# The first mixer of an encoder trunk: eight q buffers, an earlier fourth q projection, LayerNorm's scale and shift behind the spatial product, one 1/std chain for three blocks

## The chip, the cores and the metric

The kernel runs on one core of a Trainium2 chip. The metric is the device time of one execution in microseconds (us), as the median over several executions; a lower time is better. A core has a matrix engine (TensorE, PE in the profile, with its weight load as PEld), three engines for elementwise work (VectorE or DVE, ScalarE or ACT, GpSimd or POOL) and a queue from which the transfers here are issued (SyncE, SP). Each engine works through its own list of instructions in order and waits at an instruction whose operands or buffers are not there yet.

## The reference

Two groups of tokens, a prompt of 512 and a sample of 256, go through two layers with shared weights; the width is D = 1024. Each layer is a half SwiGLU, a mixer and a second half SwiGLU. The change is in the mixer of the first layer alone, which computes, with h the normed input:

```python
z = h @ w_in
zs = jax.nn.gelu(z[..., :2 * SGU_WIDTH], approximate=False)
u, vh = zs[..., :SGU_WIDTH], zs[..., SGU_WIDTH:]            # 512 each
vh = layer_norm(vh, sgu_ln_g, sgu_ln_b)                     # (x - mu) * rsqrt(var + EPS) * g + b
vh = vh.reshape(B, nc, BLOCK, SGU_GROUPS, SGU_GROUP_DIM)    # blocks of 128 tokens, 4 groups of 128
vmix = jnp.einsum('gij,bnjgc->bnigc', sgu_w, vh) + jnp.transpose(sgu_b)[None, None, :, :, None]
a_out = u * vmix.reshape(B, L, SGU_WIDTH)
...
b_out = window_gqa(rope_partial(q), rope_partial(k), v, sink)
return jnp.concatenate([a_out, b_out], axis=-1) @ w_out
```

`window_gqa` is attention of 8 query heads over 2 key and value heads (kv 0 and 1): each block of 128 queries looks at its own block and its two neighbours within its group, through a mask, with a softmax that has one more term for each head, the sink. The results are float32 and must be exact to about that.

## The kernel before, in words

**Arithmetic.** A float32 operand is split into a rounded high part and a rest ("hi" and "lo": `split`, L194 to L197, a cast on ACT at L196 and a subtraction on DVE at L197). A product takes three matmuls, hi with hi, hi with lo, lo with hi (`mm3`, L176), all issued at L140. One such group of three is called a step below. `proj` (L183) makes a projection as eight steps, one for each 128 rows of D. Weights arrive as `raw` by DMA on the SP queue (L92) and are split in halves of 512 columns into `whi` (ACT, L114) and `wlo` (DVE, L115), with five buffers of each. Transposes on PE are issued at L144.

**Layout.** All 768 tokens lie in one axis: columns 0 to 512 are the prompt (four blocks of 128), 512 to 768 the sample (two blocks). `GROUPS` cuts it there, `HALVES` in 384 and 384. PSUM has two pools with four banks each: "mm" for projections, "aux" for everything short.

**What sets the order.** PE's list is the order in which the program issues matmuls; the program keeps a virtual time `self.t`, to which each matmul adds its estimated length (L134). Side work is written as generators that yield a delay: `spawn` (L146) adds one, and `tick` (L158), called after each step, runs those whose time has come, so their matmuls stand between the steps of a projection. `run_until` and `drain` (L164, L172) step the generators at once, whatever their delay, until something is reached. The lists of ACT, DVE, POOL and SP are made by a list scheduler that takes instructions as their operands become ready by its own model of time; they are fixed in the program and do not adapt on the chip. A buffer of a pool is given out in the order of the program's requests.

**The first mixer** (`mixer0`, L927 to L1144). It loads tables (rope, mask `msk`, `sink`, LayerNorm's gain `lng` and shift `lnb`, both spread over all partitions, the spatial product's offset `sb`) and the spatial weights, which it splits into `swh` and `swl` (L952). It projects keys and values for both groups (L983). `roped` (L959) rotates a projection out of PSUM in four DVE steps with two buffers of the pool "tmp". This pool has three buffers of 128 x 512, shared by the rotation (`rt`, `ru`), the values (`vf`), the copies of value products (`tb`), the gate's tiles (`vg`), those of u (`ug`) and the raw spatial weights.

- `q_heads(m)` (L998) projects two query heads for both groups, rotates them and splits them into q tiles: for each group a pool with six buffers, of which one `q_heads` takes two (hi and lo). There are four such calls.
- `attention` (L1061) is the generator for the softmax part. For each kv and each of the six blocks it issues scores (`score`, L1008, whose softmax is `finish_rows`, L900: row maximum on DVE L907, exp on ACT L913, the sink's part L918, reciprocal, product with 1/sum on DVE L922), yields `GAP0`, issues the value product of the block before (`values`, L1048: copy on ACT, four adds on DVE), yields `GAP0` again, and transposes and splits the probabilities (`turn`, L1032). kv 0 needs the q tiles of calls 0 and 1, kv 1 those of calls 2 and 3. "Score (0,5)" is the last block of kv 0.
- `vh_part` (L1109) projects the gate half for two groups of three blocks, each block in an mm bank, with tokens as partitions. Each result goes through the exact Gelu on ACT (L1121) into a "tmp" tile, and a generator `sgu` is spawned for it.
- `sgu` (L1079) is LayerNorm and the spatial product of one block: statistics (L1082, L1085), 1/std by a chain of 13 small DVE steps (`rsqrt`, L262 to L276), then three DVE passes over 128 x 512 (subtract mean and times 1/std L1087, times gain L1090, plus shift L1091), a split (L1095), twelve matmuls of 128 columns on `swh` and `swl`, and four adds of `sb` on DVE (L1105). The delays between are `SGU`.
- `u_part` (L1124) projects the other half, multiplies by the token norm, applies Gelu and multiplies into the spatial product's result.
- The main part (L1137 to L1144) spawns the attention, calls `q_heads` 0 to 2 and `vh_part`, then steps the generators until score (0,5) has been issued (L1141), calls `q_heads(3)` and `u_part`, and ends with `mixer_out` (L821). There `ready(k)` splits the mixer's result (L833) for the output projection, six of eight tiles ahead of it, the last two after the attention has been drained.

ACT loads another function table (`ACT_TABLE_LOAD`) where its list changes between Gelu and Exp.

Of the kernel before, what the change touches and what calls it, by code (L numbers as in the profile page):

```python
# [42 lines left out]

WTOTAL = 12 * D * FF + 8 * EARLY * P * D + D * 1792 + 2 * D * D + D * 3072 + D * 512
VTOK = (4.0,9.0)
GAP0 = 5.4
SGU = (8.0, 3.0, 4.0)
NP, NQ = 16, 2
GAPS1 = (3.5, 0.6, 3.5, 0.8)
# [2 lines left out]
class Trunk:  # L52
# [874 lines left out]
    def mixer0(self):  # L927
        nc = self.nc
        mp = self.mixer_open("m0")
        self.spawn(self.norm_r(mp, False))  # L930
        xs = (self.xh, self.xl)
        tmp = lambda name: mp.tile([P, TA], F32, tag="tmp", name=name, bufs=3)
# [6 lines left out]
        nc.sync.dma_start(msk, self.aps["gmask"])  # L939
        sink = mp.tile([P, P], F32, tag="sink", name="sink")[:, :8]  # L940
        nc.sync.dma_start(sink, self.aps["sink"].partition_broadcast(P))
        lng = mp.tile([P, 512], F32, tag="lng", name="lng")
        nc.sync.dma_start(lng, self.aps["ln_g"].partition_broadcast(P))
        lnb = mp.tile([P, 512], F32, tag="lnb", name="lnb")
        nc.sync.dma_start(lnb, self.aps["ln_b"].partition_broadcast(P))
        sb = mp.tile([P, 512], F32, tag="sb", name="sb")
        nc.sync.dma_start(sb, self.aps["sgu_b"].partition_broadcast(P))
# [2 lines left out]
        swh = mp.tile([P, 4, P], F32R, tag="swh", name="swh")  # L950
        swl = mp.tile([P, 4, P], F32R, tag="swl", name="swl")
# [7 lines left out]
        def roped(ps, c0, c1):  # L959
            n = c1 - c0  # L960
            t, u = tmp("rt")[:, :n], tmp("ru")[:, :n]
            nc.vector.stream_shuffle(out=u, in_=ps[:, :n], mask=swap)
            nc.vector.tensor_tensor(out=t, in0=ps[:, :n], in1=rct[:, c0:c1], op=ALU.mult)
# [21 lines left out]
        for g in (0, 1):  # L985
            c0, c1 = GROUPS[g]
            t = roped(pkv[g][0], c0, c1)
            for h in (0, 1):
# [3 lines left out]
                out=vf[:, : c1 - c0], in0=pkv[g][1][:, : c1 - c0], in1=self.rt[:, c0:c1], op=ALU.mult  # L992
# [3 lines left out]
        ot = [self.otile(k) for k in range(KD)]  # L996

        def q_heads(m):  # L998
            qs = []
            w = self.unit("l0_w_in", 0, KD, 1024 + m * P, P)  # L1000
            for g in (0, 1):
                c0, c1 = GROUPS[g]
                t = roped(self.proj(w, xs, GROUPS[g]), c0, c1)
                qs.append([mp.tile([P, c1 - c0], F32R, tag=f"q{g}", name=f"q{g}", bufs=6) for _ in "hl"])
                self.q_split(*qs[g], t)
            qheads.append(qs)

# [51 lines left out]
        qheads, scored, gates = [], [], []  # L1059

        def attention(gap):  # L1061
            cur = None
            for kv in (0, 1):
                for n in range(6):
                    while len(qheads) < 2 * kv + 2:
                        yield 0.5
                    new = score(kv, qheads[2 * kv : 2 * kv + 2], n)
                    scored.append((kv, n))
                    yield gap
                    if cur:  # L1070
                        values(*cur[:3], tt)
                    yield gap
                    cur = new
                    tt = turn(*cur)
                    yield 0.3 * gap
            yield 1.0
            values(*cur[:3], tt)

        def sgu(n, v):  # L1079

            bs = mp.tile([P, 6], F32, tag="bs", name="bs", bufs=2)
            nc.vector.bn_stats(out=bs, in_=v)  # L1082
            mv = mp.tile([P, 8], F32, tag="mv", name="mv", bufs=2)
            it = mp.tile([P, 1], I32, tag="mvi", name="mvi", bufs=2)
            nc.vector.bn_aggr(out=mv[:, 0:2], in_=bs)  # L1085
            self.rsqrt(mv[:, 2:3], mv[:, 1:2], 1.0, mv[:, 3:4], mv[:, 4:5], it)
            nc.vector.tensor_scalar(  # L1087
                out=v, in0=v, scalar1=mv[:, 0:1], scalar2=mv[:, 2:3], op0=ALU.subtract, op1=ALU.mult
            )
            nc.vector.tensor_tensor(out=v, in0=v, in1=lng, op=ALU.mult)  # L1090
            nc.vector.tensor_tensor(out=v, in0=v, in1=lnb, op=ALU.add)  # L1091
            yield SGU[0] + n % 3 * SGU[1]
            vh = mp.tile([P, 512], F32R, tag="vhh", name="vhh", bufs=2)
            vl = mp.tile([P, 512], F32R, tag="vhl", name="vhl", bufs=2)
            self.split(vh, vl, v)  # L1095
            yield SGU[2]
            ps = self.psum(self.aux, "aux")
            for g in range(4):
                c = slice(g * P, (g + 1) * P)
                self.mmul(ps[:, c], vh[:, c], swh[:, g, :], True, False)  # L1100
                self.mmul(ps[:, c], vh[:, c], swl[:, g, :], False, False)
                self.mmul(ps[:, c], vl[:, c], swh[:, g, :], False, True)
            for g in range(4):
                c = slice(g * P, (g + 1) * P)
                nc.vector.tensor_tensor(  # L1105
                    out=ot[g][:, n * P : (n + 1) * P], in0=ps[:, c], in1=sb[:, c], op=ALU.add
                )

        def vh_part():  # L1109
            for n0 in (0, 3):  # L1110
                ps = [self.psum() for _ in range(3)]
                for k in range(KD):
                    if k % 2 == 0:
                        w = self.unit("l0_w_in", k, 2, 512, 512)
                    for i in range(3):
                        a, b = (n0 + i) * P, (n0 + i + 1) * P
                        st = (self.xh[k][:, a:b], self.xl[k][:, a:b])
                        self.mm3(ps[i], st, w[k % 2], k == 0, k == KD - 1)
                for i in range(3):
                    v = tmp("vg")  # L1120
                    nc.scalar.activation(v, ps[i], AF.Gelu, scale=self.ry[:, n0 + i : n0 + i + 1])  # L1121
                    gates.append(self.spawn(sgu(n0 + i, v)))

        def u_part():  # L1124
            for m in range(4):
                w = self.unit("l0_w_in", 0, KD, m * P, P)
                for g in (0, 1):
# [6 lines left out]
                        self.drain(c)  # L1134
                    nc.vector.tensor_tensor(out=ot[m][:, c0:c1], in0=ot[m][:, c0:c1], in1=u, op=ALU.mult)

        att = self.spawn(attention(GAP0))  # L1137
        for m in range(3):
            q_heads(m)
        vh_part()  # L1140
        self.run_until(lambda: (0, 5) in scored)  # L1141
        q_heads(3)
        u_part()
        self.mixer_out("l0_w_out", ot, att)  # L1144
# [350 lines left out]
def trace(nc, phases=PHASES):  # L1495

    aps = {}
    inp = lambda n, s: aps.__setitem__(n, nc.dram_tensor(f"in_{n}", s, F32, kind="ExternalInput").ap())
    inp("x", (KD, P, T))
    inp("w", (WTOTAL,))  # L1500
    inp("gains", (P, KD * len(NORMS)))
    inp("rope", (2, P, TA))
    inp("gmask", (P, 3 * P))
    inp("nmask", (P, NMASK))
    inp("sink", (8,))
    inp("ln_g", (512,))
# [12 lines left out]

def layout(units, i):  # L1520
    x = np.concatenate([i["x_prompt"][0], i["x_sample"][0]], axis=0)
    w = np.zeros(WTOTAL, np.float32)
    off = 0
    for name, k0, nk, c0, n in units:
        size = P * nk * n
        w[off : off + size].reshape(P, nk, n)[...] = (
            i[name][k0 * P : (k0 + nk) * P, c0 : c0 + n].reshape(nk, P, n).transpose(1, 0, 2)
        )
        off += size
    rpb = np.zeros((16, 15, RPB_W), np.float32)  # L1530
    rpb[:, :, RPB_PAD : RPB_PAD + 31] = i["l1_rpb"]
    return {
        "in_x": np.ascontiguousarray(x.T).reshape(KD, P, T),
        "in_w": w,
        "in_gains": np.ascontiguousarray(np.concatenate([i[n].reshape(KD, P).T for n in NORMS], axis=1)),
        "in_rope": rope_tables(),
        "in_gmask": gqa_mask(),
        "in_nmask": natten_masks(),
        "in_sink": np.ascontiguousarray(i["l0_sink"]),
        "in_ln_g": np.ascontiguousarray(i["l0_sgu_ln_g"]),  # L1540
        "in_ln_b": np.ascontiguousarray(i["l0_sgu_ln_b"]),
        "in_sgu_b": np.ascontiguousarray(i["l0_sgu_b"].reshape(512)),
        "in_sgu_w": np.ascontiguousarray(i["l0_sgu_w"].transpose(2, 0, 1)),
        "in_rpb": rpb,
    }
# [21 lines left out]
```

## Time and profile before

| what | value |
|---|---|
| three executions | 2618.2, 2620.6 and 2620.9 us, median 2620.62 |
| the profiled execution | 2616.48 us in all, 2614.7 us span of its instructions |
| granted TensorE clock, mean | 0.991 |
| DMA | 218.99 MB, mean 84 GB/s |
| first mixer's stretch from gate projection to output projection, 580 to 696 us | PE busy 105.2 of 116 us, DVE 103.7, ACT 73.8 |
| rest of the span, 0 to 580 and 696 to 2614.7 us | PE busy 2447.9 of 2498.7 us |

All moments are microseconds from the start of the profiled span. A row of an instruction gives its start, its length in us, the engine, the line of the kernel, the operation, what it writes and reads by the program's names, its shape and how many of the same kind follow each other in the row; in brackets stands the time that the engine was idle just before and the instruction that ended this wait. A row of a group starts with its line and gives the count, then shortest, middle and longest length in ns, and the stretch in which they lie. A matmul's length is modelled and overlaps the next one, so that the step from one start to the next is the better measure of its cost. The granted clock is the TensorE clock as a share of full speed.

### The profile page before, as it was taken

Reading aid. Unit: us, or ns where it says so; the run is one execution under the profiler, and the core shown is the slowest. Engines: PE = TensorE matmul, PEld = TensorE weight load, DVE = VectorE, ACT = ScalarE, POOL = GpSimd, SP = SyncE. Lnnn points to the kernel's source line nnn. Section 1 sums busy time; section 2 is a strip of 40 time slices with the busy share of each in tenths; the row PEclk is TensorE's granted clock in tenths of the full one; section 3 lists DMA queues with packets and bytes.
Section 4 is the critical chain, followed back from the end, with each engine's and each line's share of the span. In section 5 each row is a group of like instructions: output and inputs, shape, how many; then the busy total and the mean of one; then the engine's idle time right before and its main releaser. Section 6 shows DMA issues by size and latency. Waiting matters only on the chain.

```text
span 2614.7 us, 41195 instructions
## 1 busy us (share of the span) xinstructions
PE 2553.1 (98%) x15094; PEld 2488.8 (95%) x15094; DVE 2264.1 (87%) x4793; ACT 1366.3 (52%) x2851; POOL 88.4 (3%) x172
## 2 busy tenths in 40 slices
PE   7999999998999999999999999999999999999997
PEld 7999999987899999999999999989898999999997
DVE  8998899889779989889999888986677699988897
ACT  7544454555655545445654445454445475444543
POOL 0000000000100000000000000001222100000000
PEclk9999999999999999999999999999999999999999
DMA  5333222421223322222322222232221332222221
GB/s 172 112 112 95 81 65 65 160 73 45 82 77 97 97 65 81 66 81 81 97 81 81 74 72 73 72 129 63 63 64 40 106 99 88 81 73 73 73 69 69
DMA packets 83898, 218.99 MB, mean 84 GB/s; under 512 B 20080, under 2 KB 32880, under 8 KB 83696
## 3 DMA queue, kind: packets, MB, share of 16 engines
q1 hardware_dynamic: 83552, 216.34, 26.3%
q8 instruction: 118, 1.93, 0.3%
q14 instruction: 84, 0.69, 0.1%
q10 hardware_dynamic: 144, 0.03, 0.0%
HBM read 206.90 MB, written 15.07 MB: 85 GB/s over the span
## 4 chain that ended last, share of the span: by engine, by line
PE 88%; DVE 8%; ACT 2%; issue 1%; DMA 1%; SPq 0%; DVEq 0%; ACTq 0%
PE ps_mm L140 55%; PE ps_aux L140 32%; DVE wlo L115 1%; PE ps_aux L144 1%; DMA raw<-in_w 1%; DVE xl L741 1%; ACT p L913 1%; DVE p L922 0%; DVE p L907 0%; DVE tl L197 0%; DVE tmp L362 0%; ACT xh L740 0%; DVE x L708 0%; DVE ol L197 0%; ACT whi L114 0%
## 5 line engine op out<-in xcount | busy, mean ns | idle before, releaser
L114 ACT CAST whi<-s 128x512 fp32r<-128x512 f32 x496 | 305.1, 620 | 413.7 <-DVE s L611 169.9
L114 ACT CAST whi<-raw 128x512 fp32r<-128x512 f32 x512 | 311.4, 618 | 232.5 <-PE ps_mm L140 98.7
L115 DVE TENSOR_TENSOR wlo<-s,whi 128x512 fp32r<-128x512 f32 x496 | 337.4, 686 | 56.3 <-ACT whi L114 53.9
L115 DVE TENSOR_TENSOR wlo<-raw,whi 128x512 fp32r<-128x512 f32 x494 | 337.7, 691 | 24.9 <-ACT whi L114 20.7
L140 PE MATMUL ps_mm<-db,whi 128*128 128x384 f32 x864 | 219.3, 334 | 0.4 <-DVE sg L508 0.4
L140 PE MATMUL ps_aux<-dt,whi 128*128 128x384 f32 x864 | 219.1, 334 | 0.0
L140 PEld LDWEIGHTS ps_mm<-db,whi 128*128 128x128 f32 x864 | 155.9, 188 | 0.7 <-DVE sg L508 0.7
L140 PEld LDWEIGHTS ps_aux<-dt,whi 128*128 128x128 f32 x864 | 156.0, 188 | 0.0
L140 PE MATMUL ps_mm<-xh,whi 128*128 128x512 f32 (+1 forms) x416 | 147.3, 354 | 3.6 <-ACT xh L740 3.6
L140 PE MATMUL ps_mm<-db,wlo 128*128 128x384 f32 x432 | 144.3, 334 | 0.0
L140 PE MATMUL ps_aux<-dt,wlo 128*128 128x384 f32 x432 | 144.3, 334 | 0.0
L140 PE MATMUL ps_mm<-xl,whi 128*128 128x512 f32 (+1 forms) x416 | 142.3, 342 | 1.1 <-DVE xl L741 1.1
L140 PE MATMUL ps_mm<-xh,wlo 128*128 128x512 f32 (+1 forms) x416 | 141.9, 341 | 0.0
L611 DVE TENSOR_TENSOR s<-raw,raw 128x512 f32<-128x512 f32 x124 | 84.0, 686 | 21.3 <-DMA raw<-in_w 21.1
L611 DVE TENSOR_TENSOR s<-raw 128x512 f32<-128x512 f32 x124 | 85.2, 687 | 18.6 <-DMA raw<-in_w 18.3
L499 DVE TENSOR_TENSOR u<-ps_aux,u 128x384 f32<-128x384 f32 x176 | 97.2, 552 | 4.0 <-PE ps_aux L140 3.9
L140 PE MATMUL ps_aux<-dh,whi 128*128 128x384 f32 x384 | 97.7, 335 | 0.6 <-DVE x L708 0.6
L913 ACT ACTIVATE p<-p,st 128x256 f32<-128x256 f32 (+3 forms) x144 | 68.9, 480 | 54.5 <-DVE st L911 54.4
L663 DVE TENSOR_TENSOR x<-ps_aux,x 128x384 f32<-128x384 f32 x160 | 84.9, 552 | 13.0 <-PE ps_aux L140 13.0
L140 PEld LDWEIGHTS ps_mm<-xh,whi 128*128 128x128 f32 x416 | 79.9, 192 | 13.9 <-ACT xh L740 4.7
L140 PE MATMUL ps_mm<-oh,whi 128*128 128x384 f32 x256 | 88.7, 346 | 4.6 <-DVE x L890 4.0
L663 DVE TENSOR_TENSOR x<-ps_mm,x 128x384 f32<-128x384 f32 x160 | 86.2, 551 | 5.8 <-PE ps_mm L140 5.4
(486 smaller groups left out, 8046.3 us busy)
## 6 DMA issues: line engine op xcount, KB each, us to landing
raw<-in_w SPq DMA_DIRECT2D x350, 512.0 KB, 3.7
xdm<-x SPq DMA_DIRECT2D x16, 384.0 KB, 2.3
x<-in_x SPq DMA_DIRECT2D x16, 192.0 KB, 5.4
x<-xdm SPq DMA_DIRECT2D x8, 384.0 KB, 3.3
xold<-xdm SPq DMA_DIRECT2D x8, 384.0 KB, 3.0
out_y<-y SPq DMA_DIRECT2D x8, 384.0 KB, 2.4
tab<-skew SPq DMA_DIRECT2D x8, 256.0 KB, 5.6
raw<-in_w SPq DMA_DIRECT2D x8, 256.0 KB, 2.6
```

Source lines behind the costliest of these rows:

```text
L114: nc.scalar.copy(hi, src)
L115: (eng or nc.gpsimd).tensor_tensor(out=lo, in0=src, in1=hi.bitcast(F32), op=ALU.subtract)
L140: self.nc.tensor.matmul(out, lhsT=lhsT, rhs=rhs, start=start, stop=stop, **kw)
L144: self.nc.tensor.transpose(out, src, self.ident)
L499: nc.vector.tensor_tensor(out=t, in0=bank[key, n], in1=t, op=ALU.add)
L611: f = lambda o, x, y, op: self.nc.vector.tensor_tensor(out=o, in0=x, in1=y, op=op)
L663: nc.vector.tensor_tensor(out=o, in0=ps, in1=o, op=ALU.add)
L741: nc.vector.scalar_tensor_tensor(out=lo, in0=src, scalar=gain, in1=hi.bitcast(F32), op0=ALU.mult, op1=ALU.subtract)
L913: nc.scalar.activation(outs[i], outs[i], AF.Exp, bias=nm[:, i : i + 1], accum_out=sm[:, i : i + 1])
```

## The change

- The q tiles have eight buffers for each group instead of six, so that all four calls of `q_heads` have tiles of their own. The line that waited for score (0,5) ahead of `q_heads(3)` is gone; `q_heads(3)` follows `vh_part` directly. `GAP0` is 5.2 instead of 5.4.
- LayerNorm's gain and shift leave the gate tiles. The spatial product mixes tokens, the gain and the shift belong to columns, so that W(v*g + b) = (Wv)*g + Wb. A new generator `offsets` puts the shift through the spatial product once, at the mixer's start (a split, twelve matmuls and one add into `sb`), and `sgu`'s four last steps become (product times `lng`) plus `sb`. `lng` is now an input of 128 x 4, a scalar for each partition; `lnb` is a "tmp" tile.
- The 1/std chain runs once for the three blocks of a group (`stats`, tiles of 128 x 3) and also gives nb = -mean/std. The pass that remains over each gate tile, v/std + nb, is on ACT. `sgu` is spawned for the three blocks after the common chain.

```diff
-GAP0 = 5.4
+GAP0 = 5.2
...
-        lng = mp.tile([P, 512], F32, tag="lng", name="lng")
-        nc.sync.dma_start(lng, self.aps["ln_g"].partition_broadcast(P))
-        lnb = mp.tile([P, 512], F32, tag="lnb", name="lnb")
+        lng = mp.tile([P, P], F32, tag="lng", name="lng")[:, :4]
+        nc.sync.dma_start(lng, self.aps["ln_g"])
+        lnb = tmp("lnb")
         nc.sync.dma_start(lnb, self.aps["ln_b"].partition_broadcast(P))
...
-                qs.append([mp.tile([P, c1 - c0], F32R, tag=f"q{g}", name=f"q{g}", bufs=6) for _ in "hl"])
+                qs.append([mp.tile([P, c1 - c0], F32R, tag=f"q{g}", name=f"q{g}", bufs=8) for _ in "hl"])
...
-        def sgu(n, v):
-
-            bs = mp.tile([P, 6], F32, tag="bs", name="bs", bufs=2)
-            nc.vector.bn_stats(out=bs, in_=v)
-            mv = mp.tile([P, 8], F32, tag="mv", name="mv", bufs=2)
-            it = mp.tile([P, 1], I32, tag="mvi", name="mvi", bufs=2)
-            nc.vector.bn_aggr(out=mv[:, 0:2], in_=bs)
-            self.rsqrt(mv[:, 2:3], mv[:, 1:2], 1.0, mv[:, 3:4], mv[:, 4:5], it)
-            nc.vector.tensor_scalar(
-                out=v, in0=v, scalar1=mv[:, 0:1], scalar2=mv[:, 2:3], op0=ALU.subtract, op1=ALU.mult
-            )
-            nc.vector.tensor_tensor(out=v, in0=v, in1=lng, op=ALU.mult)
-            nc.vector.tensor_tensor(out=v, in0=v, in1=lnb, op=ALU.add)
-            yield SGU[0] + n % 3 * SGU[1]
-            vh = mp.tile([P, 512], F32R, tag="vhh", name="vhh", bufs=2)
-            vl = mp.tile([P, 512], F32R, tag="vhl", name="vhl", bufs=2)
-            self.split(vh, vl, v)
+        vhl = lambda: [mp.tile([P, 512], F32R, tag=f"vh{n}", name=f"vh{n}", bufs=2) for n in "hl"]
+
+        def mixed(ps, v):
+
+            for g in range(4):
+                c = slice(g * P, (g + 1) * P)
+                self.mmul(ps[:, c], v[0][:, c], swh[:, g, :], True, False)
+                self.mmul(ps[:, c], v[0][:, c], swl[:, g, :], False, False)
+                self.mmul(ps[:, c], v[1][:, c], swh[:, g, :], False, True)
+
+        def offsets():
+
+            b = vhl()
+            self.split(*b, lnb)
+            yield VTOK[0]
+            ps = self.psum(self.aux, "aux")
+            mixed(ps, b)
+            nc.vector.tensor_tensor(out=sb, in0=ps, in1=sb, op=ALU.add)
+
+        def stats(vs):
+
+            mv = mp.tile([P, 6, 4], F32, tag="mv", name="mv", bufs=2)
+            it = mp.tile([P, 3], I32, tag="mvi", name="mvi", bufs=2)
+            for i, v in enumerate(vs):
+                bs = mp.tile([P, 6], F32, tag="bs", name="bs", bufs=2)
+                nc.vector.bn_stats(out=bs, in_=v)
+                nc.vector.bn_aggr(out=mv[:, i, 0:2], in_=bs)
+            y, nb = mv[:, 3, 0:3], mv[:, 4, 0:3]
+            self.rsqrt(y, mv[:, 0:3, 1], 1.0, nb, mv[:, 5, 0:3], it)
+            nc.vector.scalar_tensor_tensor(out=nb, in0=mv[:, 0:3, 0], scalar=-1.0, in1=y, op0=ALU.mult, op1=ALU.mult)
+            return y, nb
+
+        def sgu(n, v, y, nb):
+
+            i = n % 3
+            nc.scalar.activation(v, v, AF.Identity, scale=y[:, i : i + 1], bias=nb[:, i : i + 1])
+            yield SGU[0] + i * SGU[1]
+            vs = vhl()
+            self.split(*vs, v)
             yield SGU[2]
             ps = self.psum(self.aux, "aux")
+            mixed(ps, vs)
             for g in range(4):
                 c = slice(g * P, (g + 1) * P)
-                self.mmul(ps[:, c], vh[:, c], swh[:, g, :], True, False)
-                self.mmul(ps[:, c], vh[:, c], swl[:, g, :], False, False)
-                self.mmul(ps[:, c], vl[:, c], swh[:, g, :], False, True)
-            for g in range(4):
-                c = slice(g * P, (g + 1) * P)
-                nc.vector.tensor_tensor(
-                    out=ot[g][:, n * P : (n + 1) * P], in0=ps[:, c], in1=sb[:, c], op=ALU.add
+                nc.vector.scalar_tensor_tensor(
+                    out=ot[g][:, n * P : (n + 1) * P], in0=ps[:, c], scalar=lng[:, g : g + 1], in1=sb[:, c],
+                    op0=ALU.mult, op1=ALU.add,
                 )
...
+                vs = []
                 for i in range(3):
-                    v = tmp("vg")
-                    nc.scalar.activation(v, ps[i], AF.Gelu, scale=self.ry[:, n0 + i : n0 + i + 1])
-                    gates.append(self.spawn(sgu(n0 + i, v)))
+                    vs.append(tmp("vg"))
+                    nc.scalar.activation(vs[i], ps[i], AF.Gelu, scale=self.ry[:, n0 + i : n0 + i + 1])
+                y, nb = stats(vs)
+                for i in range(3):
+                    gates.append(self.spawn(sgu(n0 + i, vs[i], y, nb)))
...
+        self.spawn(offsets())
         att = self.spawn(attention(GAP0))
         for m in range(3):
             q_heads(m)
         vh_part()
-        self.run_until(lambda: (0, 5) in scored)
         q_heads(3)
         u_part()
         self.mixer_out("l0_w_out", ot, att)
```

More of the change, by code (lines that the diff above doesn't have):

```diff
@@ L1505, in trace @@
     inp("sink", (8,))
-    inp("ln_g", (512,))
+    inp("ln_g", (P, 4))
     inp("ln_b", (512,))
@@ L1539, in layout @@
         "in_sink": np.ascontiguousarray(i["l0_sink"]),
-        "in_ln_g": np.ascontiguousarray(i["l0_sgu_ln_g"]),
+        "in_ln_g": np.ascontiguousarray(i["l0_sgu_ln_g"].reshape(4, P).T),
         "in_ln_b": np.ascontiguousarray(i["l0_sgu_ln_b"]),
```

## The prediction

> **What bounds the kernel now.** I read the page first, then the busy time by stage, then the waits of PE, then PE's and ACT's instructions in order of time.
>
> ```profile
> PE 2553.1 (98%) x15094; PEld 2488.8 (95%) x15094; DVE 2264.1 (87%) x4793; ACT 1366.3 (52%) x2851; POOL 88.4 (3%) x172
> ```
>
> PE (TensorE) works in 2553.1 of 2614.7 us; its matmuls hardly change here, so the time moves by PE's waits. Busy time in stretches of the first mixer (columns: PE, PEld, DVE, ACT, POOL with their counts, granted clock, DMA share, GB/s):
>
> ```profile
> 580.00:611.00 31.00, 29.77 (x171) 24.66 (x170) 30.70 (x123) 20.04 (x43) 0.00 (x0) 1.00 0.17 52
> 611.00:623.00 12.00, 5.17 (x25) 3.71 (x24) 12.00 (x57) 7.52 (x17) 0.00 (x0) 0.65 0.15 44
> 623.00:649.00 26.00, 25.50 (x160) 22.40 (x161) 23.04 (x89) 11.24 (x30) 0.00 (x0) 0.97 0.04 12
> 649.00:686.00 37.00, 35.97 (x226) 30.70 (x226) 28.82 (x79) 25.34 (x53) 2.59 (x2) 1.00 0.17 54
> 686.00:696.00 10.00, 8.79 (x44) 7.31 (x43) 9.16 (x25) 9.70 (x22) 1.51 (x2) 1.00 0.53 163
> ```
>
> The hole is 611 to 623: PE works 5.17 of 12 us, DVE all 12, and the granted clock is 0.65. From 580 to 611 PE runs with DVE full beside it. What PE waits for in the hole:
>
> ```profile
> 617.53 2.03 PE L144 MATMUL ps_aux<-ident,p 128*128 128x128 f32 x8 [5.74 <-DVE p L922]
> ...
> 619.49 0.58 PE L140 MATMUL ps_aux<-kh,q 64*128 64x256 f32 x1
> ...
> 621.16 0.58 PE L140 MATMUL ps_aux<-kh,q 64*128 64x256 f32 x1 [1.09 <-DVE tl L197]
> ...
> 622.74 0.79 PE L140 MATMUL ps_mm<-xh,whi 128*128 128x512 f32 x1
> ...
> 624.91 0.40 PE L140 MATMUL ps_mm<-xh,wlo 128*128 128x512 f32 x1
> ...
> 632.33 0.33 PE L140 MATMUL ps_aux<-swh,vhl 128*128 128x128 f32 x1 [0.50 <-DVE vhl L197]
> ```
>
> This is line 1141: the fourth q projection waits until score (0,5) is out, so softmax, transposes and split stand alone in PE's queue.
>
> **The change part by part.** Times are in the profiled run of before (span 2614.7, 2616.5 us in all, 4.1 under the median 2620.6; I add the sum to either).
>
> 1. *The hole goes.* Undisturbed, eight transposes and twelve scores take:
>
> ```profile
> 605.04 1.04 PE L144 MATMUL ps_aux<-ident,p 128*128 128x128 f32 x8
> ...
> 605.84 0.48 PE L140 MATMUL ps_mm<-whi,xh 128*128 128x512 f32 x1
> ...
> 639.48 0.39 PE L140 MATMUL ps_aux<-kh,q 64*128 64x256 f32 x2
> ...
> 640.39 0.50 PE L140 MATMUL ps_mm<-xh,whi 128*128 128x512 f32 x1
> ...
> 764.75 0.34 PE L140 MATMUL ps_mm<-oh,whi 128*128 128x384 f32 x1
> ...
> 764.92 0.34 PE L140 MATMUL ps_mm<-ol,whi 128*128 128x384 f32 x1
> ```
>
> 0.80 (605.04 to 605.84) and 0.91 (639.48 to 640.39); matmuls of 384 columns follow each other by 0.17 (764.75 to 764.92), so those of 512 by 0.23. In the hole: waits 5.74 + 1.09 + 0.50; transposes 617.53 to 619.49, 1.16 too long; scores 621.16 to 622.74, about 0.75 too long; five 512-wide matmuls 622.74 to 624.91, 2.17 where five steps of 0.23 make 1.13, 1.04 too long. Sum **-10.3**. With eight q tiles nothing holds the projection back, and the changed program indeed puts its matmuls right behind the gate projection.
>
> 2. *The offset product* adds twelve 128-wide matmuls early, where PE never waits, so nothing hides them. Its price is that of one block's product:
>
> ```profile
> 596.48 0.22 PE L140 MATMUL ps_aux<-swh,vhh 128*128 128x128 f32 x1
> ...
> 597.77 0.45 PE L140 MATMUL ps_mm<-whi,xh 128*128 128x512 f32 x1
> ```
>
> **+1.3.** Its cast, split and add (about 0.6 each) lie on ACT and DVE while both wait for the norm; were that cover gone, they would cost up to 2:
>
> ```profile
> 524.27 0.96 DVE L957 TENSOR_TENSOR rct<-rct,rt 128x768 f32<-128x768 f32 x1 [2.16 <-ACT rt L819]
> ```
>
> The SP queue issues as many DMAs as before; lng's is smaller. Cost 0 (bounds 0 and +0.5).
>
> 3. *LayerNorm.* It removes three DVE passes for each of six blocks and four of six 1/std chains:
>
> ```profile
> L1121 ACT ACTIVATE vg<-ps_mm,sm x6: 689/690/690, 579.0 to 611.0; 128x512 f32<-128x512 f32 x6
> ...
> L1087 DVE TENSOR_SCALAR vg<-vg,mv x6: 539/542/546, 585.8 to 627.4; 128x512 f32<-128x512 f32 x6
> ...
> L1090 DVE TENSOR_TENSOR vg<-vg,lng x6: 664/685/689, 586.8 to 628.2; 128x512 f32<-128x512 f32 x6
> ...
> L196 ACT CAST vhh<-vg x6: 619/621/640, 590.1 to 630.2; 128x512 fp32r<-128x512 f32 x6
> ```
>
> 6 x (0.54 + 0.69 + 0.69) = 11.5 us of DVE (the add of L1091 has the shape of L1090), against six ACT passes (not in the trace; between the cast's 0.62 and the Gelu's 0.69). That takes DVE off the limit from 580 to 611 and with it PE's waits there, 31.00 - 29.77 = **-1.2**. The last pass with a gain for each partition I take at the old add's time; a tenth of it more would be hidden.
>
> 4. *What is late next: the second Gelu.* In before the three Gelus of a group follow each other, and PE's first matmul into the second bank they free (third bank of the next group) comes just after:
>
> ```profile
> 578.99 0.69 ACT L1121 ACTIVATE vg<-ps_mm,sm 128x512 f32<-128x512 f32 x1
> ...
> 580.39 1.43 ACT L1121 ACTIVATE vg<-ps_mm,sm 128x512 f32<-128x512 f32 x2 [0.71 <-PE ps_mm L140]
> ...
> 582.34 1.28 ACT L913 ACT_TABLE_LOAD   x1
> ...
> 583.64 0.62 ACT L913 ACTIVATE p<-p,st 128x384 f32<-128x384 f32 x1
> ```
>
> ```profile
> 582.24 0.39 PE L140 MATMUL ps_mm<-whi,xh 128*128 128x512 f32 x1
> ```
>
> The changed program can be built and its lists read, without times. GAP0, 5.2 for 5.4, only moves attention's steps in these lists, and is in them. ACT's list has at this place (x3: three more alike):
>
> ```
> L1141 LoadActFuncSet
> L1141 Activation vg<-ps_mm_6222,sm 128x512
> L913 LoadActFuncSet
> L913 Activation p,st<-p,st 128x384
> L913 Activation p,st<-p,st 128x384 x3
> L918 Activation st<-st 128x4
> L1141 LoadActFuncSet
> L1141 Activation vg<-ps_mm_6223,sm 128x512
> ```
>
> The second Gelu now stands behind the exps of score (0,2) and two table loads. The mm pool has four banks, one is free, so the next group's third bank needs the second Gelu. First Gelu at about 579.5 (the place where before had 580.39, one step of three matmuls, 0.68, and a small wait sooner); + 0.69 + 1.28 + 4 x 0.62 + 0.2 + 1.28 + 0.69 = 586.1. PE wants the bank at about 582.0 (582.24 in before). **+4.0** (bounds +3 and +5). Behind it score (0,3) needs the bank of values (0,1), whose copy stands on ACT behind the three new passes and two casts and on DVE behind the chain: PE would wait 2.4, or nothing if it comes late itself; I take **+1.4**.
>
> 5. *The second group's LayerNorm.* The rows nearest to what stands in its way:
>
> ```profile
> 610.80 0.48 DVE L907 CUSTOM_DVE_ANT_0 p<-ps_aux,msk,sink 128x256 f32<-128x256 f32 x1
> ...
> 617.04 1.14 DVE L922 TENSOR_SCALAR p<-p,st 128x256 f32<-128x256 f32 x4
> L963 DVE TENSOR_TENSOR rt<-ps_mm,rct x10: 403/550/684, 526.6 to 639.8; 128x512 f32<-128x512 f32 x5, 128x256 f32<-128x256 f32 x5
> ```
>
> In the changed DVE list the last step of the chain stands behind the first row maximum of score (0,5), which PE delivers only between the u projection's first matmuls. From there: maximum 0.48, step 0.2, three ACT passes at 0.6 to 0.69, cast 0.62, split 0.69, about 4.0; PE has nine matmuls of 0.23, 2.0, to fill it: wait 2.0. The second block's cast stands behind a table load (1.28), four exps and a copy (about 0.5 each), and its split behind value adds and rotation steps, some 5.4 after the first; PE has 3.4: wait 2.0. The third split stands behind the softmax products (1.14), three rotation steps of 512 (0.68), four of 256 (0.40) and two gate outputs (an estimate of 0.25 each), 5.3; PE has the rest of a block's product and six matmuls, 2.4: wait 2.9. These also delay the rotation of the fourth q, since three gate tiles hold all three "tmp" buffers. Sum **+6.9** (bounds +4 and +9).
>
> 6. *Entry of the output projection.* In before its splits are spread; the changed list has twelve in a row, behind the last u and four value adds:
>
> ```profile
> 686.67 2.90 DVE L197 TENSOR_TENSOR ol<-o,oh 128x384 fp32r<-128x384 f32 x6
> ...
> 693.42 0.44 PE L140 MATMUL ps_mm<-oh,whi 128*128 128x384 f32 x1 [0.56 <-ACT oh L196]
> ...
> 694.22 0.44 PE L140 MATMUL ps_mm<-ol,whi 128*128 128x384 f32 x1 [0.35 <-DVE ol L197]
> ```
>
> Each takes 0.48. PE's fifth step needs the ninth: 2.8 + 9 x 0.48 = 7.1 after the last u projection, where it would be at 2.2; about 5.2 in all. Before loses 1.2 in 686 to 696 (10.00 - 8.79) and 1.0 in 649 to 686: **+2.9**, bounds 0 and +4; and the 0.9 that before lost at score (1,3) (part of that 1.0) is in it. The last values land only 3 matmuls ahead of the late products, but these first need tokens under 384, split long before: 0.
>
> Sum: -10.3 + 1.3 - 1.2 + 4.0 + 1.4 + 6.9 + 2.9 = 5.0; PE arriving later at 5 and 6 than assumed shortens these waits by about 1: **+4**.
>
> *The clock.* A short wait has been followed by slow matmuls, and an equal one not:
>
> ```profile
> 759.94 0.44 PE L140 MATMUL ps_mm<-oh,whi 128*128 128x384 f32 x1 [1.79 <-DVE x L890]
> ...
> 761.60 0.52 PE L140 MATMUL ps_mm<-oh,wlo 128*128 128x384 f32 x1
> ...
> 761.91 0.52 PE L140 MATMUL ps_mm<-oh,whi 128*128 128x384 f32 x1
> ...
> 2100.50 0.44 PE L140 MATMUL ps_mm<-oh,whi 128*128 128x384 f32 x1 [1.77 <-DVE x L890]
> ```
>
> From 761.3 on, eleven matmuls step by 0.31 (761.60 to 761.91) instead of 0.17: a spell costs 1.6. [...] I count no spell in the sum, because behind waits 4 and 5 PE would meet the next wait anyway; the rest is a rival.
>
> **The rivals.**
> - *A, the hole closes and nothing takes its place.* The exps of score (0,2) are done before 582, or the bank isn't needed then, and DVE, 11.5 us lighter, delivers in time: -10.3 + 1.3 - 1.2 = -10.2, of which about 1 is lost at wait 6: -9, 2611.6. For it: DVE was full from 580 to 623, and that load goes. Against it: ACT's order is fixed in the program, and an exp can't precede its scores. Chance 0.22.
> - *B, the new waits slow the clock.* Waits of 2 to 4 us stand ahead of stretches full of matmuls at three places (behind 4, 5 and 6); each spell costs 1.6 as at 759.94: 4 + 3 x 1.6, about +9, 2629.6. It decides from one spell on: +4 + 1.6 is past 5.2. For it: clock 0.65 in 611 to 623, and 759.94. Against it: 2100.50, where 1.77 us did nothing, and that a slow PE meets the next wait later. Chance 0.30.
> - *C, the change doesn't do what it says:* the projection's matmuls move, but its rotation waits for the gate tiles' buffers, so that the softmax after it stands alone in its turn; with 6 hidden, gain and new waits cancel: +1, 2621.6. Chance 0.10.
> - *Forecast*: waits 4 to 6 as sized, +4, **2624.6**, with its own range 2620 to 2628. Chance 0.38.
>
> **How the numbers follow.** A measurement of this kernel tells about 0.2% (5.2 us) from no change, so same is 2615.4 to 2625.9. Faster: A without its slowest tenth, 0.20. Slower: B and the upper quarter of the forecast (waits at their upper bounds), 0.40. Same: the rest, 0.40. The range leaves out the outer half of A and B's top: 2613 to 2633.
>
> **What would show it.** 1: no wait of PE on p L922 above 2 us at score (0,4)'s transposes. 4: PE waits for a Gelu, 3 to 5 us, once, at the start of the second gate group; wrong if under 1. 5: three waits on the gate's casts and splits, 2 us each. 6: a string of waits on ol of 4 to 5 us. Clock: granted clock under 0.9 in more than one stretch of this mixer means B, 1.0 throughout the forecast or A. If all waits are missing, A is right and my reading of the lists' order wrong.

## The result, and the profile after

The changed kernel takes 2624.6 us (median of 9 executions, 2622.3 to 2628.5), the kernel before 2619.3 beside it (median of 9). The ratio after to before is 1.0024, with a 95% interval of 1.0016 to 1.0033: slower by some 0.24%, about 6 us. One of before's nine executions took 3152.4 us, and the ratio goes by the others alone. The profiled execution took 2623.47 us, 2620.8 of them span. That the median is the forecast one (2624.6) to the tenth is chance: the forecast was +4 on a before of 2620.6, and measured is +5.3 on one of 2619.3. The rest asks whether it came about as forecast.

The changed kernel's busy time in the stretches of the prediction (same columns):

```profile
580.00:611.00 31.00, 26.98 (x141) 22.25 (x140) 22.39 (x76) 20.68 (x42) 0.00 (x0) 0.89 0.22 68
611.00:623.00 12.00, 12.00 (x67) 9.88 (x66) 9.06 (x30) 9.72 (x19) 0.00 (x0) 1.00 0.14 46
623.00:649.00 26.00, 21.26 (x117) 18.59 (x116) 20.53 (x70) 12.67 (x26) 0.00 (x0) 0.82 0.04 11
649.00:686.00 37.00, 36.64 (x219) 30.64 (x219) 26.71 (x78) 26.85 (x55) 3.04 (x2) 0.99 0.14 43
686.00:696.00 10.00, 7.28 (x39) 6.26 (x38) 8.68 (x21) 7.90 (x19) 1.90 (x1) 0.83 0.36 103
```

The hole of 611 to 623 is gone (PE busy 12.00 of 12, before 5.17), and DVE is no longer full. Instead three stretches have lost PE time and clock together: 580 to 611 (26.98, clock 0.89), 623 to 649 (21.26, 0.82) and 686 to 696 (7.28, 0.83). PE's waits from 500 to 800 us (columns: total, times, longest):

```profile
PE ps_mm L140 <- ACT vg L1141: 4.0, 1, 4.0
PE ps_aux L140 <- DVE vhl L197: 2.8, 3, 2.4
PE ps_mm L140 <- DVE ol L197: 2.7, 1, 2.7
...
PE ps_aux L140 <- ACT vhh L196: 1.9, 1, 1.9
```

These are the places of the forecast's steps 4 (vg), 5 (vhh, vhl) and 6 (ol). What stands behind the first is seen in PE's and ACT's rows:

```profile
585.75 0.80 PE L140 MATMUL ps_mm<-whi,xh 128*128 128x512 f32 x1 [3.97 <-ACT vg L1141]
586.35 0.63 PE L140 MATMUL ps_mm<-wlo,xh 128*128 128x512 f32 x1
...
591.47 0.57 PE L140 MATMUL ps_mm<-wlo,xh 128*128 128x512 f32 x1
591.87 0.40 PE L140 MATMUL ps_mm<-whi,xl 128*128 128x512 f32 x1
```

```profile
579.10 0.69 ACT L1141 ACTIVATE vg<-ps_mm,sm 128x512 f32<-128x512 f32 x1 [0.73 <-PE ps_mm L140]
579.81 1.28 ACT L913 ACT_TABLE_LOAD   x1
581.11 0.62 ACT L913 ACTIVATE p<-p,st 128x384 f32<-128x384 f32 x1
...
583.72 1.28 ACT L1141 ACT_TABLE_LOAD   x1
585.01 1.26 ACT L1141 ACTIVATE vg<-ps_mm,sm 128x512 f32<-128x512 f32 x2
```

ACT takes the first Gelu, loads Exp, does four exps, loads Gelu again and only then frees the bank. Then PE's matmuls of 512 columns step by 0.43 (586.35 to 591.47 is 12 steps) until 591.9, where the same shape steps by 0.23 ahead of this stretch (557.39 to 557.62): from 585.75 to 591.87 it is 14 steps in 6.12 instead of 3.2, a spell that costs 2.9.

The second group and the entry of the output projection, on PE:

```profile
631.34 0.33 PE L140 MATMUL ps_aux<-swh,vhh 128*128 128x128 f32 x1 [1.92 <-ACT vhh L196]
...
632.07 0.33 PE L140 MATMUL ps_aux<-swh,vhl 128*128 128x128 f32 x1 [0.29 <-DVE vhl L197]
...
637.68 0.33 PE L140 MATMUL ps_aux<-swh,vhl 128*128 128x128 f32 x1 [0.16 <-DVE vhl L197]
...
643.00 0.47 PE L140 MATMUL ps_aux<-swh,vhl 128*128 128x128 f32 x1 [2.37 <-DVE vhl L197]
...
690.61 0.53 PE L140 MATMUL ps_mm<-ol,whi 128*128 128x384 f32 x1 [2.72 <-DVE ol L197]
```

Three of these waits have a spell behind them too: worked out from the steps of their rows as above, about 1.8 (632.7 to 636.3), 3.3 (643.0 to 649.8) and 1.7 (690.6 to 694.3). With the first that is 9.7 us lost to slow matmuls, beside 11.4 of waits (3.97 + 4.74 + 2.72). The granted clock agrees: it is 0.50 from 585.00 to 591.83, 632.79 to 636.20, 643.03 to 649.86 and 690.82 to 694.23, 20.48 us together, and 1.00 in the rest of this mixer. In the kernel before it is 0.50 for 10.24 us there, from 614.49 to 624.73.

To compare single profiled executions without what differs ahead of the mixer and behind it, I take the **mixer's stretch**: from the transposes of the values to the moment PE begins to wait for x (L890; L898 where lines moved). In the changed kernel:

```profile
533.81 0.60 PE L144 MATMUL ps_aux<-ident,vf 128*128 128x128 f32 x4
...
557.15 0.40 PE L140 MATMUL ps_mm<-whi,xh 128*128 128x512 f32 x1
...
766.70 0.44 PE L140 MATMUL ps_mm<-oh,whi 128*128 128x384 f32 x1 [1.78 <-DVE x L890]
766.98 0.34 PE L140 MATMUL ps_mm<-ol,whi 128*128 128x384 f32 x1
767.16 0.34 PE L140 MATMUL ps_mm<-oh,wlo 128*128 128x384 f32 x1
```

and in the kernel before:

```profile
535.46 0.60 PE L144 MATMUL ps_aux<-ident,vf 128*128 128x128 f32 x4
...
557.50 0.40 PE L140 MATMUL ps_mm<-whi,xh 128*128 128x512 f32 x1
```

After: 766.70 - 1.78 - 533.81 = 631.11. Before: 759.94 - 1.79 - 535.46 = 622.69. So the mixer is 8.4 longer in these two executions. In the table, before's median is that of the first row's session; beside e1 to e4 it was 2618.6, beside e5 to e8 2618.8 and beside e9 to e11 2617.3, so across these groups the ratios compare better than the medians.

| kernel | median, us | ratio to before, interval | mixer's stretch, us |
|---|---|---|---|
| before | 2619.3 | | 622.69 |
| changed | 2624.6 | 1.0024, 1.0016 to 1.0033 | 631.11 |
| e1_gap54 | 2616.1 | 0.9989, 0.9980 to 0.9998 | 619.86 |
| e2_gelu_first | 2617.7 | 0.9999, 0.9990 to 1.0008 | 618.46 |
| e3_q_only | 2619.9 | 1.0004, 0.9995 to 1.0013 | 623.21 |
| e4_ln_only | 2617.9 | 1.0000, 0.9991 to 1.0009 | 623.85 |
| e5_warm | 2624.4 | 1.0024, 1.0015 to 1.0033 | 628.68 |
| e6_halves_gelu | 2617.1 | 0.9990, 0.9981 to 0.9998 | 618.22 |
| e7_gap63 | 2627.4 | 1.0027, 1.0017 to 1.0038 | 630.06 |
| e8_halves_gap63 | 2625.8 | 1.0026, 1.0017 to 1.0035 | 629.20 |
| e9_late12 | 2609.3 | 0.9969, 0.9958 to 0.9980 | 614.33 |
| e10_late12_halves | 2609.1 | 0.9967, 0.9954 to 0.9979 | 613.80 |
| e11_q_only_late12 | 2610.5 | 0.9977, 0.9966 to 0.9988 | 618.01 |

### The profile page after: what moved, and what is told of

Read it like the earlier page. It is cut to its first block, busy times and chain, and to the rows that moved or that the text cites. A ratio compares the mean times of both kernels' runs of the same rounds, so it can differ in the third digit from the quotient of the medians.

```text
span 2620.8 us, 41172 instructions
## 1 busy us (share of the span) xinstructions
PE 2557.9 (98%) x15106; PEld 2491.5 (95%) x15106; DVE 2256.9 (86%) x4727; ACT 1375.2 (52%) x2862; POOL 90.3 (3%) x172
## 4 chain that ended last, share of the span: by engine, by line
PE 89%; DVE 7%; ACT 3%; issue 1%; DMA 1%; SPq 0%; DVEq 0%; ACTq 0%
PE ps_mm L140 55%; PE ps_aux L140 32%; PE ps_aux L144 1%; DVE wlo L115 1%; DMA raw<-in_w 1%; ACT p L913 1%; DVE xl L741 1%; ACT whi L114 0%; DVE p L907 0%; DVE p L922 0%; DVE tl L197 0%; ACT xh L740 0%; ACT sq L219 0%; DVE x L708 0%; DVE ol L197 0%
```

## The experiments

The theory is that the change's gain is lost where attention's steps stand ahead of the gate's and of u's in the lists of ACT and DVE, and in the slow matmuls behind those waits ("order theory"). Its rivals are that a part of the change costs this by itself, and that the slow matmuls have another cause.

**e1 and e2: the order on ACT.**

```diff
-GAP0 = 5.2
+GAP0 = 5.4
```

> The changed kernel with GAP0 at 5.4 again; nothing else differs. In ACT's list the three Gelus of the first gate group then follow each other, ahead of the exps of score (0,2). Order theory (the change loses its gain where attention's steps stand ahead of the gate's on ACT and DVE): the wait of 3.97 us for vg and the slow matmuls behind it (2.9 us by their steps in the changed kernel's trace) are gone, 7 us or more less than the changed kernel's 2624.6: 2614 to 2618. Rival (a part of the change costs this by itself, wherever attention stands, and PE meets it at the next wait): 2622 to 2627, with a wait of PE of 3 us or more elsewhere between 580 and 660.

For e2, with GAP0 5.2:

```diff
-                    nc.scalar.activation(vs[i], ps[i], AF.Gelu, scale=self.ry[:, n0 + i : n0 + i + 1])
+                    with self.tc.high_priority():
+                        nc.scalar.activation(vs[i], ps[i], AF.Gelu, scale=self.ry[:, n0 + i : n0 + i + 1])
```

> The changed kernel (GAP0 5.2) with the three Gelus of each gate group put ahead of everything else that is ready, so that ACT takes them before the exps of score (0,2). Order theory: no wait for vg, 6 to 8 us less than 2624.6: 2616 to 2619; the exps are 1.4 us later, which nobody waits for. Rival that the exps' delay comes back as a wait of the transposes on the softmax product: 2621 to 2624. Rival that a part costs by itself: 2622 to 2627.

Both came out as the order theory has it: 2616.1 and 2617.7. ACT in e1:

```profile
581.03 0.69 ACT L1141 ACTIVATE vg<-ps_mm,sm 128x512 f32<-128x512 f32 x1
582.44 1.43 ACT L1141 ACTIVATE vg<-ps_mm,sm 128x512 f32<-128x512 f32 x2 [0.72 <-PE ps_mm L140]
...
584.40 1.28 ACT L913 ACT_TABLE_LOAD   x1
```

No PE wait for vg is left in either, nor more than 0.7 for vhl. Both mend the order of the second gate group too: its three Gelus follow each other there (from 610.77 in e1), while in the changed kernel a table load for Exp stands behind the first of them (614.95) and the other two begin at 619.73. So these runs don't tell whether the second group's waits came from its own order or from the first group's delay. The smallest edit of the change, GAP0 from 5.4 to 5.2, costs 8.5 us (2624.6 to 2616.1; 0.35% by the ratios): it puts score (0,2) one step of the gate projection earlier, ahead of the last step of the first block instead of behind it, and on ACT its exps then follow the first Gelu. With GAP0 left at 5.4 the change is 0.1% faster than before, at the edge of what can be measured.

In both, the entry of the output projection is what remains. e1's rows on PE, then on ACT:

```profile
680.47 0.69 PE L140 MATMUL ps_mm<-oh,whi 128*128 128x384 f32 x1 [3.45 <-ACT oh L196]
```

```profile
677.37 1.28 ACT L1154 ACT_TABLE_LOAD   x1
678.67 0.93 ACT L1154 ACTIVATE ug<-ug 128x512 f32<-128x512 f32 x2
679.51 3.80 ACT L196 CAST oh<-o 128x384 fp32r<-128x384 f32 x9
```

The last two Gelus of u stand behind the exps of score (1,2), and nine of the twelve splits behind them.

**e3 and e4: each half of the change alone.** e3 is the kernel before with `bufs=8` and without its line 1141; e4 is the changed kernel with that line, `bufs=6` and GAP0 5.4.

> The kernel before with eight q buffers and the projection of the fourth q pair directly behind the gate projection; LayerNorm, its shift and GAP0 as before. If the hole is all that the place of the projection costs, 10.3 us less than before's 2619.3: 2608 to 2611. If DVE is the bound (it was full from 580 to 623), its surplus only moves to the next wait and the gain is 2 to 5: 2614 to 2617. If the earlier projection is itself the loss: above 2620.

> The changed kernel with six q buffers, the wait for score (0,5) ahead of the fourth projection and GAP0 5.4: only LayerNorm's part differs from before. By the forecast's terms: +1.3 for the offset product, -1.2 for the waits of 580 to 611, and a hole that DVE, 11.5 us lighter by its passes, ends 2 to 5 us sooner: 2615 to 2618. If LayerNorm's part costs by itself (three ACT passes in a row, a chain that waits for three blocks): above 2621.

e3: 2619.9, between the second case and the third. The hole is gone, but DVE is still full from 580 to 623, as in the second case: PE waits 3.9 for vhl. At the entry it waits 3.4 for ACT (oh), as in e1. With spells of 2.8 and 3.1 behind them these take the whole gain. e4: 2617.9 is in the range of the forecast's terms, but the hole doesn't end sooner: PE waits 5.1 for p and 2.6 for tl there (5.7 and 1.1 before), and the mixer's stretch is 1.2 longer than before. Neither half is a loss by itself beyond the measurement, which speaks against that rival, and neither is a gain beyond it.

**e5: the slow matmuls.**

```diff
+                        if n0 and k == 0 and i == 2:
+                            idle = self.psum(self.aux, "aux")
+                            for r in range(14):
+                                nc.tensor.matmul(
+                                    idle, lhsT=self.xh[0][:, 0:P], rhs=self.xh[1][:, 0:512], start=r == 0, stop=r == 13
+                                )
```

> The changed kernel with fourteen matmuls of 512 columns, whose result nobody reads, put ahead of the one that waits 3.97 us for vg; all else in the same order. If the slow matmuls behind that wait (0.43 a step instead of 0.23 from 585.75 to 591.9, 2.9 us lost) come from PE standing idle, the remaining wait is about 1 us (3.97 less 14 steps of 0.23), the steps behind it are 0.23 and the time is about 2.9 less than the changed kernel's 2624.6: 2621 to 2623. If they come from something else (operands, the engines beside), the steps behind stay at 0.43 and the time at 2624 to 2626.

```profile
583.18 3.33 PE L1138 MATMUL ps_aux<-xh,xh 128*128 128x512 f32 x14
587.31 0.50 PE L140 MATMUL ps_mm<-whi,xh 128*128 128x512 f32 x1 [0.79 <-ACT vg L1147]
587.65 0.39 PE L140 MATMUL ps_mm<-wlo,xh 128*128 128x512 f32 x1
587.88 0.39 PE L140 MATMUL ps_mm<-whi,xl 128*128 128x512 f32 x1
...
597.17 0.38 PE L140 MATMUL ps_aux<-kh,q 64*128 64x256 f32 x1 [0.74 <-DVE tl L197]
598.34 0.35 PE L140 MATMUL ps_aux<-kh,q 64*128 64x256 f32 x1 [0.79 <-DVE o L1054]
```

The steps behind the wait are 0.23 (587.65 to 587.88) and no longer 0.43: with PE at work for 3.33 us of the wait this spell is gone, the case that the expectation has for PE standing idle. The time missed the expectation: 2624.4 against 2621 to 2623. The 2.9 us came back in part. At score (0,3) PE now waits 0.74 and 0.79, 1.5 in all, where the changed kernel waits for nothing, and at the second group's second split 1.28 instead of 0.16. The later spells are shorter too: the granted clock is 0.50 for 6.83 us of this mixer (645.05 to 648.46 and 689.42 to 692.83) instead of 20.48. The mixer's stretch is 2.4 shorter in the profiled execution, and the medians differ by only 0.2; which of the two is nearer, these runs don't settle, nor what the fourteen matmuls alone are worth.

**e6: the order of the splits.** With e2's edit, in `mixer_out` for the first mixer:

```diff
-        for k in early:
-            ready(k)
+        for c0, c1 in HALVES:
+            for k in early:
+                self.split(oh[k][:, c0:c1], ol[k][:, c0:c1], ot[k][:, c0:c1])
```

> The kernel with the Gelus put first (2617.7 before), and at the entry of the first mixer's output projection the six splits of the first half of the tokens ahead of the six of the second half, where tile by tile they were twelve in a row of which the first half's product needs every other one. If the entry is bound by the splits' order: the wait of 2.7 for ol stays as long as the first split does, but the steps behind it are no more held up: 1 to 2.5 us less, 2615 to 2616.7. If it is bound by the last u's Gelu and multiplication alone: 2617 to 2618, and the slow steps behind the wait are the clock's.

2617.1, the second case: the wait is still 2.69. What is late is not the ninth split but the first. Why shows on DVE, here in the changed kernel (e2 and e6 have the same sequence):

```profile
688.46 1.17 DVE L1054 TENSOR_TENSOR o<-ps_aux,tb 64x128 f32<-64x128 f32 x4
689.66 0.43 DVE L1157 TENSOR_TENSOR o<-o,ug 128x256 f32<-128x256 f32 x1
690.00 5.71 DVE L197 TENSOR_TENSOR ol<-o,oh 128x384 fp32r<-128x384 f32 x12
```

All twelve subtractions stand behind four value adds and the last product with u, and PE starts at 690.61 when the first is done. The order among the twelve can hardly count here, since PE is slow behind the first: three matmuls of 0.32 (690.61 to 690.93 is one step) take as long as two splits of 0.48.

**e7 and e8: attention farther apart.** GAP0 6.3, and the same with e6's order.

> The changed kernel with GAP0 at 6.3: attention's steps stand farther apart. In ACT's list all Gelus of a gate group follow each other, the passes of the second group stand ahead of score (0,5)'s exps, the last Gelus of u stand ahead of the exps of their neighbour score, and 16 table loads are left of 22. Order theory: none of the waits for vg, vhh, vhl and oh above 1.5 us, no slow matmuls behind them: 12 to 16 us less than 2624.6, 2609 to 2613. Rival: what is gained there comes back at the mixer's end, where more scores are left to be drained alone: a wait there of 4 us or more and 2615 to 2620.

> The kernel with GAP0 6.3, and the splits ahead of the output projection ordered by halves. 0 to 1.5 us less than with GAP0 6.3 alone if its entry still waits for splits, the same if it doesn't.

My expectation for e7 was wrong. Its rival was right in what happens and too low in size, 2615 to 2620: e7 takes 2627.4, more than before. The waits for vg and at the entry are gone, but one for vhl is 4.0, and at the mixer's end the last scores' softmax stands alone in PE's queue twice (waits of 4.16 and, at 738.67, 4.15), as in the hole of before, with the granted clock at 0.50 from 728.35 to 742.00:

```profile
728.91 2.02 PE L144 MATMUL ps_aux<-ident,p 128*128 128x128 f32 x8 [4.16 <-DVE p L922]
```

e8 took 2625.8, 1.6 less than e7, within the spread of its interval.

**e9 to e11: one score out of the way.** The changed kernel with GAP0 5.4 and, in `attention`:

```diff
+                    if (kv, n) == (1, 2):
+                        yield 4.0
                     new = score(kv, qheads[2 * kv : 2 * kv + 2], n)
```

> The changed kernel with GAP0 5.4 and a single delay of 4 us in attention ahead of score (1,2); in ACT's list the last Gelu of u and the splits of the output projection then stand ahead of that score's exps. If the entry (a wait of 3.45 us for oh and 3.2 us of slow matmuls at GAP0 5.4) is late because the last Gelu stands behind those exps, both go: 5 to 7 us less than 2616.1, 2609.5 to 2611.5. If the 4 us come back where the last scores are drained, as at GAP0 6.3 (two waits of 4.2 us there): 2614 to 2618.

> The same with the splits ahead of the first output projection ordered by halves: 0 to 1.5 us less than without, since the first half's product then needs the first six splits and no longer every other one of twelve; the same if PE doesn't wait for splits there any more.

> The kernel before with eight q buffers, the earlier fourth projection and the delay of 4 us ahead of score (1,2), LayerNorm as before. The entry's wait (3.44 us and 3.1 us of slow matmuls there without the delay) goes: 2612.5 to 2615 from 2619.9. DVE then still holds the second group's splits (waits of 3.9 us for vhl and 2.8 us of slow matmuls), which LayerNorm's part takes away: so 3 to 6 us above the kernel with both parts and the same delay. If LayerNorm's part is worth nothing, the two are within 1.5 us.

e9 takes 2609.3, ratio 0.9969 (0.9958 to 0.9980): 0.2 under its range, less than both kernels, and less than e1 by 6.8 (0.20% by the ratios, 5.5 us by the mixer's stretch). On ACT the last Gelu now stands ahead of the exps:

```profile
671.65 0.41 ACT L1156 ACTIVATE ug<-ug 128x256 f32<-128x256 f32 x1
...
678.66 1.28 ACT L913 ACT_TABLE_LOAD   x1
```

and of PE's waits from 500 to 800 us none of the mixer's own is above 0.7 (the first two rows, the waits for x and for the next norm, are in all kernels):

```profile
PE ps_mm L140 <- DVE x L890: 2.0, 2, 1.8
PE ps_aux L140 <- DVE diag L256: 1.2, 1, 1.2
...
PE ps_aux L140 <- DVE vhl L197: 0.7, 1, 0.7
```

One spell is left, with the granted clock at 0.50 from 633.20 to 636.62. The order of the splits (e10) adds nothing that can be told: 2609.1. e11, with LayerNorm as before, takes 2610.5, less than the 2612.5 to 2615 expected: 1.3 more than e9 by the medians, where 3 to 6 were expected and up to 1.5 was to mean nothing, and 3.7 by the mixer's stretch. Its waits for vhl (3.9, with a spell of 2.8) are there as expected. The same pair without the delay, e1 and e3, differs by 3.8 and 3.4. The ratios' intervals overlap in both pairs, so how much LayerNorm's part is worth stays open between nothing and some 4 us.

## Why the prediction was right, point by point

The number held, and so did the places of the large waits; the bookkeeping between waits and clock did not, and that its errors cancelled is in part luck.

1. *The hole goes, -10.3:* right. Score (0,4)'s transposes wait for nothing, and 611 to 623 is full. e3 shows the same for the edit alone.
2. *The offset product, +1.3:* right. From the values' transposes to the gate's first matmul it is 22.04 before (535.46 to 557.50) and 23.34 after (533.81 to 557.15).
3. *LayerNorm:* DVE goes from 30.70 to 22.39 busy in 580 to 611, and the small waits there are gone in the changed kernel. In e1, without the shift of step 4, 0.95 of the 1.23 is still lost there (PE 30.05 of 31), so the term of -1.2 was not LayerNorm's alone. Two of its prices were low: the pass on ACT takes 0.80 (0.62 to 0.69 assumed), the output's add with a gain 0.34 against the old add's 0.28.
4. *The second Gelu, +4.0:* measured 3.97, by the very sequence worked out from the list. *Score (0,3), +1.4:* absent in the changed kernel, 1.5 in e5. "Or nothing if it comes late itself" was the case: the spell made PE late, and without it (e5) the wait is there.
5. *The second group, +6.9:* 1.92 + 0.29, 0.16 and 2.37 are 4.7, where 2.0, 2.0 and 2.9 were forecast; the second is hardly a wait. In e5, where PE is less late, they are 1.9, 1.3 and 2.4 with small ones beside, 6.1 in all (4.0 for vhl, 2.1 for vhh).
6. *The entry, +2.9:* the size is about right (2.72 and a spell of 1.7, less 2.1 that before lost at these places: 2.3), the mechanism only in part. The place was right: the twelve splits do stand behind the last u and four value adds. But PE waits for the first of them and then, slow, for none, where "PE's fifth step needs the ninth" had it; e6 shows no gain from another order. (The forecast's own rows make 7.1 - 2.2 = 4.9, not 5.2.) At GAP0 5.4 the first split is late for another reason, the last Gelus of u behind the exps of score (1,2) on ACT: the delay that moves them (e9) removes the wait.
7. *The clock, 0 in the sum:* this is the step that failed. "I count no spell in the sum" - four of the new waits were followed by a spell, 9.7 us in all, more than the three times 1.6 of rival B. By the prediction's own sign, a granted clock under 0.9 in more than one stretch (0.89, 0.82 and 0.83), this is B. In part the reason given for leaving spells out holds: a slow PE meets the next wait later, and the waits came out shorter than forecast (at 4 and 5 by 1.4 and 2.2). But that is less than half of what the spells cost. e5 shows that trade in part: with the first spell of 2.9 taken out, 1.5 and 1.1 came back as waits.

Together, by these measured sizes: -10.3 + 1.3 - 1.2 + 4.0 + 2.9 + 4.7 + 5.1 + 2.3 = 8.8, against 8.4 of the mixer's stretch. The whole spans differ less, by 6.1: the changed kernel's profiled execution reached the mixer 1.65 sooner, and its wait for x had no spell behind it (766.98 to 767.16 is a step of 0.17), where before's had one of 1.6. The medians differ by 5.3. So for the mixer of these two executions the forecast of +4 is short by half, and part of why the time came out right lies outside the mixer; whether that part is in most executions these two profiles don't tell.

The mechanism that I had as the forecast and the one that I had as rival B both took place, and each ate a part of the other. Rival A (nothing takes the hole's place) is nearly what e9 is: 8.1 under before, where A had 9 under; it needed attention's place set right at two points. Rival C was not the case.

## What to carry to other kernels

An engine that works a fixed list makes the place of a side task a cost of its own: here 0.2 us of a planner's gap was worth more than three dropped passes over six tiles. Before pricing what an edit saves, read the changed lists at each point where a buffer or bank is handed on, ACT's changes of function table above all (1.28 us for a load here), and ask what stands ahead of the instruction that frees it. And add up waits and slow-clock spells as one account: in e5 a spell was taken out and waits came back in its place.

## What the runs showed of the hardware

- PE's matmuls ran at about half pace after some waits (0.43 instead of 0.23 for 512 columns, 0.32 instead of 0.17 for 384), in the changed kernel's mixer four times, for 3.4 or 6.8 us of granted clock 0.50. With fourteen matmuls put into the wait of 3.97, the steps behind it were 0.23 (e5).
- Whether a wait has such a spell behind it isn't told by its length alone. The wait for x in the first mixer is 1.77 to 1.80 in all 13 kernels; it had a spell in before, e1, e3 and e7 and none in the other nine. In the second layer, PE's rows of e9, where 3.43 us had none (steps of 0.18):

```profile
2119.54 0.41 PE L140 MATMUL ps_mm<-b110h,whi 128*128 128x384 f32 x1 [3.43 <-DVE sg L508]
2119.79 0.34 PE L140 MATMUL ps_mm<-b110l,whi 128*128 128x384 f32 x1
2119.97 0.35 PE L140 MATMUL ps_mm<-b110h,wlo 128*128 128x384 f32 x1
```

- The granted clock tells more. In each of the 13 traces it changes only on a grid of 3.41 us, whose first point lies from 0.1 to 3.3 us behind the start of the span. Two stretches of the grid in the changed kernel, then three in e9 (length, PE's busy time, and the clock third from the end):

```profile
629.38:632.79 3.41, 1.20 (x10) 1.02 (x9) 1.31 (x5) 3.38 (x5) 0.00 (x0) 1.00 0.00 0
632.79:636.20 3.41, 3.41 (x12) 2.93 (x12) 2.29 (x9) 3.38 (x12) 0.00 (x0) 0.50 0.00 0
...
2114.59:2118.01 3.42, 1.51 (x9) 1.19 (x7) 3.42 (x8) 3.36 (x8) 0.00 (x0) 1.00 0.00 0
2118.01:2121.42 3.41, 1.88 (x11) 1.91 (x12) 3.41 (x8) 2.83 (x4) 0.00 (x0) 1.00 0.41 102
2121.42:2124.83 3.41, 3.41 (x21) 3.41 (x20) 3.27 (x7) 2.36 (x6) 0.00 (x0) 1.00 0.35 84
```

The changed kernel's wait of 1.92 lies in one stretch (idle for 2.21 in all), and the next has half the clock. In e5 the same waits of 1.92 and 0.29 lie across two, with 1.29 us in the first, and have no spell. The wait of 3.43 in e9 lies across two as well, 1.90 in the first and 1.53 in the second, and no spell follows. Counted over the 13 traces, from 60 us to the last 4 us of the span: of the stretches at full clock, all 36 in which PE was idle for more than 1.90 us were followed by one at half clock, 11 of the 17 with 1.73 to 1.90 us, and 4 of the 9521 with less; in the traces of before and of the changed kernel these are 9 of 9, 1 of 2 and none of 1463. The 4 of the 9521 have 0.67 to 0.75 us of idle time among transposes, scores or spatial products; what sets them off stays open.

Each kernel has one trace here, so whether a kernel's spells stand behind the same waits in each of its executions was not shown.
